# Eight experts' two-layer products on one core: x of four experts in one load, wider transposes, evictions moved to ScalarE

## The chip, the core and the metric

The kernel runs on one core of a Trainium2 chip. A core has TensorE (PE, with a part of its own for loading weights, PEld), VectorE (DVE), ScalarE (ACT), GpSimd (POOL) and SyncE (SP), each with its own instruction queue that is worked off in order, and 16 DMA engines that move data between HBM and the on-chip memory SBUF. Transfers are issued by SP, ACT or POOL. Those from SP and ACT are called hardware_dynamic in the profile (queues q1 and q10), those from POOL software_dynamic (queue q0); in this kernel POOL's transfers of x and of the weights read fp32 and write fp16. Matrix products are summed in PSUM, from where ACT or DVE copies them out.

The metric is the time of one execution in microseconds. A separate profiled execution gives the trace; its span, from the first to the last instruction, is somewhat shorter than the time measured around it.

## What is computed

```python
n_experts, capacity, hidden, expert_hidden = 8, 256, 512, 2048
h = np.matmul(x, w1) + b1[:, np.newaxis, :]
h = np.maximum(h, 0)
return (np.matmul(h, w2) + b2[:, np.newaxis, :]).astype(np.float32)
```

x is 8 x 256 x 512 (4 MB in fp32), w1 is 8 x 512 x 2048 and w2 8 x 2048 x 512 (32 MB each), the output 4 MB. Each weight is used for 256 tokens of one expert only.

## The kernel before

**Tiles.** Everything is multiplied in fp16. POOL's transfers read fp32 weights and write fp16: `load_w1(e)` (line 82) and `load_w2(e)` (line 88) fill [128, 8192] tiles of 2 MB each, from pools of three buffers (lines 48 and 49); the w2 of experts 6 and 7 is loaded in two halves. Weight rows lie on partitions so that each partition reads one contiguous piece of HBM.

**First product.** `first_product(e)` (line 114) makes hT, the hidden layer with hidden units on partitions: for each of 16 groups j, four matmuls of 128x256 into a PSUM tile `ph` (line 121), then one ACT activation with bias and Relu into hT (line 128). It needs x transposed, xT (two buffers), which `transposes(e)` (line 95) makes on DVE in blocks of 32x32, and b1T, the bias b1 transposed by DVE (line 208). The transposes of expert e + 1 are put into the program after the activation j = 8 of expert e (line 135).

**Second product.** `second_product(e)` (line 166) runs three experts later (LAG = 3): for each of two token blocks, a bias matmul with a row of ones (line 171) and 16 matmuls of 128x512 (line 178) into `po0` and `po1`. `store` (line 142) evicts: DVE copies po0 (line 156), ACT copies po1 (line 157). For experts 0 to 3 and 4 to 5 the results are gathered in one tile each, so that a partition holds tokens of one expert that are neighbours in HBM (8 and 4 of them); these two stores are issued by POOL after all weights (`flush`, line 138). Experts 6 and 7 are stored by SP and ACT (line 164). A gathered expert's tokens are evicted in `split` parts of 128/`split` partitions: four of 32 partitions, or two of 64.

**x.** Experts 0 and 1 come by two SP loads of 512 KB in fp32 (line 190), two tokens (4 KB) to a partition, and DVE casts each (line 201). Experts 2 and 3 come by one POOL load, with four tokens to a partition, and experts 4 to 7 by another, with eight (`load_x`, line 72, with `X_LOADS`). The number of tokens on a partition, R, gives the form of the transposes: with R = 2 DVE transposes 32x256 and writes neighbours (line 109); with R = 4 it is 32x256 written at a step of two elements, with R = 8 32x512 at a step of four (line 112). Because the columns of xT then stand in another order than the rows of the output want, the activation at line 128 reads `ph` at a step of `split` and writes hT in runs.

**Order.** PE's matmuls and POOL's transfers keep the order of the program. The main loop (line 227) puts, for step s, the first product of expert s and the second of expert s - 3. The list `ring` (line 215) tells at which step POOL's transfers are put: w1 of expert s and w2 of expert s - 3 at step s - 2, with x loads ahead of w1. POOL's queue is thus: w1 of expert 0, b2, b1, w1 of 1, x of 2 and 3, w1 of 2; then w1 of 3 (which needs the buffer of expert 0, so the end of its first product), w2 of 0, x of 4 to 7; then w1 of 4, w2 of 1, and so on to w2 of 7 and the two flushes. DVE's queue at the start is: the cast and the transposes of expert 0, the cast of expert 1, seven of its transposes, the four transposes of b1T, the rest. ACT's first activation waits for b1T, and its table of functions is loaded after that wait.

Of the kernel before, what the change touches and what calls it, by code (L numbers as in the profile page):

```python
# [10 lines left out]
def kernel(  # L11
# [9 lines left out]
    nc = tc.nc  # L21
    fp32 = mybir.dt.float32
    fp16 = mybir.dt.float16
    E, T, H = x.shape
    M = w1.shape[2]
    P = 128
    nTB = T // P
    nKC = H // P
    nJ = M // P
    B = 32  # L30
    nB = P // B
# [5 lines left out]
    HALVED = (E - 2, E - 1)  # L37


    PARTS = {E - 2: ((0, 25, False), (25, 121, True), (121, 128, False))}  # L40
    nXF32 = 2
    X_LOADS = {2: 2, 4: 4}

    def ordered(ins):
        return tc.keep_in_program_order(ins)
# [3 lines left out]
    w2_pool = ctx.enter_context(tc.tile_pool(name="w2", bufs=3))  # L49
    x_pool = ctx.enter_context(tc.tile_pool(name="xp", bufs=1))  # L50
# [3 lines left out]
    out_pool = ctx.enter_context(tc.tile_pool(name="outp", bufs=2))  # L54
# [3 lines left out]
    ones1 = singles.tile([1, P], fp16)  # L58
# [4 lines left out]
    x16 = [None] * E  # L63
    xT = [None] * E
    w1_sb = [None] * E
    w2_sb = [None] * E
    hT = [None] * E
    pending = {}
    results = {}
    group_of = {first + i: (first, n) for first, n in GROUPS.items() for i in range(n)}  # L70

    def load_x(first, n):

        R = n * T // P
        t = x_pool.tile([P, R, H], fp16, tag=f"x{first}", name=f"x{first}")
        ordered(nc.gpsimd.dma_start(  # L76
            out=t, in_=x[first : first + n].rearrange("e (p r) h -> (e p) r h", r=R)
        ))
        for i in range(n):
            x16[first + i] = (t, i * (P // n), R)  # L80

    def load_w1(e):
        w1_sb[e] = w1_pool.tile([P, nKC, M], fp16, tag="w1", name="w1sb")
        ordered(nc.gpsimd.dma_start(  # L84
            out=w1_sb[e], in_=w1[e].rearrange("(p kc) m -> p kc m", kc=nKC)
        ))

    def load_w2(e):
# [3 lines left out]
        for lo in range(0, nJ, half):  # L92
            ordered(nc.gpsimd.dma_start(out=w2_sb[e][:, lo : lo + half], in_=src[:, lo : lo + half]))  # L93

    def transposes(e):


        t, p0, R = x16[e]
        n = R // nTB
        xT[e] = xT_pool.tile([P, nKC, T], fp16, tag="xT", name="xT")  # L100
        for g in range(T // R // B):
            src = t[p0 + B * g : p0 + B * (g + 1)]
            for b in range(nB):
                block = src[:, :, b * (H // nB) : (b + 1) * (H // nB)].rearrange(
                    "p (n tb) (i kc) -> p tb kc n i", tb=nTB, kc=nKC)
                out = xT[e][b * B : (b + 1) * B].rearrange(
                    "p kc (tb g i n) -> p tb g kc n i", tb=nTB, i=B, n=n)
                if n == 1:
                    nc.vector.transpose(out=out[:, :, g, :, 0, :], in_=block[:, :, :, 0, :])  # L109
                    continue  # L110
                for tb in range(nTB):
                    nc.vector.transpose(out=out[:, tb, g], in_=block[:, tb])  # L112

    def first_product(e):
        hT[e] = hT_pool.tile([P, nJ, T], fp16, tag="hT", name="hT")
        split = group_of[e][1] if e in group_of else 1
        for j in range(nJ):
            bias_at = j * B + e * nB + nB - 1
            ph = psum_h.tile([P, T], fp32, tag="ph", name="ph")
            for kc in range(nKC):  # L120
                ordered(nc.tensor.matmul(  # L121
                    out=ph,
                    lhsT=w1_sb[e][:, kc, :].rearrange("p (q j) -> p q j", j=nJ)[:, :, j],
                    rhs=xT[e][:, kc, :],
                    start=(kc == 0),
                    stop=(kc == nKC - 1),
                ))
            nc.scalar.activation(  # L128
                out=hT[e][:, j, :].rearrange("p (tb k i) -> p tb k i", tb=nTB, k=split),
                in_=ph.rearrange("p (tb i k) -> p tb k i", tb=nTB, k=split),  # L130
                func=mybir.ActivationFunctionType.Relu,
                bias=b1T[:, bias_at : bias_at + 1],
                scale=1.0,
            )
            if j == nJ // 2 and e + 1 < E:
                transposes(e + 1)
# [5 lines left out]
    def store(e, po):  # L142
        if e in group_of:
            first, n = group_of[e]
            split, rows = n, P // n
            if e == first:
                results[e] = group_pool.tile(
                    [P, split * nTB, H], fp32, tag=f"out{e}", name=f"out{e}")
        else:
            first, n, split, rows = e, 1, 1, P  # L150
            results[e] = out_pool.tile([P, nTB, H], fp32, tag="out", name="out")
        out_sb = results[first]
        at = (e - first) * rows
        for k in range(split):
            part = slice(k * rows, (k + 1) * rows)
            nc.vector.tensor_copy(out=out_sb[at : at + rows, k * nTB, :], in_=po[0][part])  # L156
            nc.scalar.copy(out=out_sb[at : at + rows, k * nTB + 1, :], in_=po[1][part])  # L157
        dst = out[first : first + n].rearrange("e (p r) h -> (e p) r h", r=split * nTB)
        if e in group_of:
            if e == first + n - 1:  # L160
                pending[first] = (dst, out_sb)
            return
        for p0, p1, scalar in PARTS.get(e, ((0, P, False),)):
            (nc.scalar if scalar else nc.sync).dma_start(out=dst[p0:p1], in_=out_sb[p0:p1])

    def second_product(e):
        po = []
        for tb in range(nTB):
            t = psum_o.tile([P, H], fp32, tag=f"po{tb}", name=f"po{tb}")
            po.append(t)  # L170
            ordered(nc.tensor.matmul(  # L171
                out=t, lhsT=ones1, rhs=b2_sb[0:1, e * H : (e + 1) * H], start=True, stop=False,
            ))
        half = nJ // 2 if e in HALVED else nJ
        for lo in range(0, nJ, half):
            for tb in range(nTB):
                for j in range(lo, lo + half):
                    ordered(nc.tensor.matmul(  # L178
                        out=po[tb],
                        lhsT=hT[e][:, j, tb * P : (tb + 1) * P],  # L180
                        rhs=w2_sb[e][:, j, :],
                        start=False,
                        stop=(j == nJ - 1),
                    ))
        store(e, po)

    x32 = []
    for e in range(nXF32):
        x32.append(out_pool.tile([P, nTB, H], fp32, tag="out", name="x32"))
        nc.sync.dma_start(out=x32[e], in_=x[e].rearrange("(p tb) h -> p tb h", tb=nTB))  # L190
    load_w1(0)
    ordered(nc.gpsimd.dma_start(  # L192
        out=b2_sb,
        in_=b2.rearrange("e h -> (e h)").rearrange("(o f) -> o f", o=1),
    ))
    ordered(nc.gpsimd.dma_start(out=b1_rows, in_=b1.rearrange("e (b i) -> (e b) i", b=nB)))  # L196
    nc.vector.memset(ones1, 1.0)  # L197

    for e in range(nXF32):
        t = x_pool.tile([P, nTB, H], fp16, tag=f"x{e}", name=f"x{e}")  # L200
        nc.vector.tensor_copy(out=t, in_=x32[e])  # L201
        x16[e] = (t, 0, nTB)
        if e == 0:
            transposes(e)


    for b in range(nB):
        nc.vector.transpose(  # L208
            out=b1T[b * B : (b + 1) * B, nB - 1 - b : nB - 1 - b + nJ * B],
            in_=b1_rows.rearrange("r (i j) -> r j i", j=nJ),  # L210
# [4 lines left out]
    ring = []  # L215
    for s in range(1, E + LAG - 1):
        if s < E:
            if s in X_LOADS:
                ring.append((s - 2, load_x, (s, X_LOADS[s])))
            ring.append((s - 2, load_w1, (s,)))  # L220
        if s >= LAG:
            ring.append((s - 2, load_w2, (s - LAG,)))
# [4 lines left out]
    for s in range(E + LAG):  # L227
        while ring and ring[0][0] <= s:
            _, put, args = ring.pop(0)
            put(*args)  # L230
        if s < E:
            first_product(s)
        if s >= LAG:
            second_product(s - LAG)
# [31 lines left out]
```

## Time and profile before

| | |
|---|---|
| time, median of 3 runs | 181.92 us (181.6 to 182.36) |
| span of the profiled execution | 179.8 us |
| mean granted TensorE clock | 0.932 |
| PE busy / DVE busy / ACT busy / POOL busy | 129.0 / 87.8 / 70.2 / 13.4 us |
| HBM read / written | 71.39 / 4.19 MB |
| moved by the DMA engines (as written) | 40.56 MB |

How to read the lines shown below. The slices are 40 equal parts of the span (or of a window), and each digit is the busy share in tenths, 9 for 90% or more. A line of the timeline gives the start in us, the duration in us, the engine, the line of the code, the operation, output and input with their shapes, how many instructions of one kind stand together, and in brackets how long the engine had been idle and what released it. SPq, POOLq and ACTq are the queues that issue transfers. A line of a group gives the count, the busy time in us and the mean of one in ns, then the idle time before them in us and its releasers. A line of a DMA queue gives the packets, the MB written and the share of the time of 16 engines that these packets took; a packet counts in the window in which it starts, so a short window can show more than 100%.

### The profile page before, as it was taken

How to read it: one execution, taken by the hardware profiler on the slowest of the kernel's cores; microseconds unless marked ns; L12 is line 12 of the kernel's file. 1: busy time of each engine (PE TensorE's matmuls, PEld its weight loads, DVE VectorE, ACT ScalarE, POOL GpSimd, SP SyncE). 2: the span in 40 equal slices, each digit the busy share in tenths (PEclk: the TensorE clock that was granted, in tenths of full speed). 3: DMA queues.
4: the chain of work that ended last, by engine and by line, in shares of the span. 5: the costliest groups of instructions: out<-in, count | busy, mean ns of one | idle time of the engine just before them, and what ended most of it. 6: DMA issues, size and time to landing. Idle time of an engine off the chain costs nothing.

```text
span 179.8 us, 1957 instructions
## 1 busy us (share of the span) xinstructions
PE 129.0 (72%) x784; PEld 86.2 (48%) x784; DVE 87.8 (49%) x125; ACT 70.2 (39%) x151; POOL 13.4 (7%) x28
## 2 busy tenths in 40 slices
PE   0005199959995930999869597969788887999740
PEld 0004089948993410794369244943387433343310
DVE  1999933985000199999999998000600020301010
ACT  0000569947993050482189005940298020111010
POOL 7000003020201010001000001000100020020000
PEclk9999999987999995599999799996999999999995
DMA  5999999999999999999999999999999999999995
GB/s 215 252 230 195 233 208 201 233 228 200 215 231 193 219 230 222 197 226 230 208 204 230 219 200 226 230 211 200 230 219 201 226 211 208 217 211 221 324 456 215
DMA packets 3828, 40.56 MB, mean 226 GB/s; under 512 B 460, under 2 KB 476, under 8 KB 1132
## 3 DMA queue, kind: packets, MB, share of 16 engines
q0 software_dynamic: 3232, 38.35, 96.5%
q1 hardware_dynamic: 476, 1.70, 2.4%
q10 hardware_dynamic: 112, 0.39, 0.5%
q8 instruction: 6, 0.10, 0.2%
q14 instruction: 2, 0.02, 0.0%
HBM read 71.39 MB, written 4.19 MB: 420 GB/s over the span
## 4 chain that ended last, share of the span: by engine, by line
DMA 55%; PE 32%; ACT 3%; another core or an unknown queue 3%; POOL 2%; issue 1%; POOLq 0%; ACTq 0%
DMA w1sb<-in_w_dram 43%; PE po L178 16%; PE ph L121 15%; DMA w2sb<-in_w_dram 12%; ACT out L157 3%; PE po L171 1%; POOL w1sb L84 1%; ACT hT L128 1%; POOL w2sb L93 0%; POOL x L76 0%; POOL b_sb L192 0%; POOL b_rows L196 0%; POOLq L250 0%; ACTq L128 0%
## 5 line engine op out<-in xcount | busy, mean ns | idle before, releaser
L121 PE MATMUL ph<-xT,w1sb 128*128 128x256 f16 x512 | 64.9, 293 | 34.1 <-DMA w1sb<-in_w_dram 21.5
L121 PEld LDWEIGHTS <-w1sb 128*128 128x128 f16 x512 | 59.8, 147 | 40.1 <-DMA w1sb<-in_w_dram 31.8
L178 PE MATMUL po<-w2sb,hT 128*128 128x512 f16 x256 | 60.0, 394 | 9.8 <-DMA w2sb<-in_w_dram 9.8
L112 DVE STREAM_TRANSPOSE xT<-x 32x256 f16<-32x256 f16 (+1 forms) x64 | 53.0, 888 | 26.0 <-DMA x<-in_x_dram 19.2
L128 ACT ACTIVATE hT<-ph,b1T 128x256 f16<-128x256 f32 x128 | 56.2, 474 | 14.4 <-PE ph L121 14.2
L178 PEld LDWEIGHTS <-hT 128*128 128x128 f16 x256 | 25.5, 101 | 44.1 <-issue 17.8
L156 DVE COPY out<-po 32x512 f32<-32x512 f32 (+2 forms) x22 | 15.1, 688 | 53.7 <-PE po L178 53.5
L157 ACT COPY out<-po 32x512 f32<-32x512 f32 (+2 forms) x22 | 12.7, 579 | 68.8 <-PE po L178 68.6
L109 DVE STREAM_TRANSPOSE xT<-x 32x256 f16<-32x256 f16 x32 | 14.0, 436 | 0.5
L93 POOL DMA_DIRECT2D w2sb<-in_w_dram x10 | 5.3, 534 | 71.6 <-PE po L178 71.6
L84 POOL DMA_DIRECT2D w1sb<-in_w_dram x8 | 4.8, 601 | 64.1 <-PE ph L121 63.3
L128 ACT ACT_TABLE_LOAD x1 | 1.3, 1283 | 20.1 <-DVE b1T L208 20.1
L171 PE MATMUL po<-b_sb,ones 1*128 1x512 f16 x16 | 4.8, 379 | 0.0
L208 DVE STREAM_TRANSPOSE b1T<-b_rows 32x512 f32<-32x512 f32 x4 | 4.1, 1031 | 0.1
L201 DVE CAST x<-x 128x1024 f16<-128x1024 f32 x2 | 1.4, 694 | 3.1 <-DMA x<-in_x_dram 3.1
L171 PEld LDWEIGHTS <-ones 1*128 1x128 f16 x16 | 0.9, 92 | 2.1 <-issue 2.1
L140 POOL DMA_DIRECT2D out_dram<-out x2 | 1.1, 538 | 9.8 <-ACT out L157 9.8
L76 POOL DMA_DIRECT2D x<-in_x_dram x2 | 1.1, 552 | 0.0
L197 DVE MEMSET ones<- 1x128 f16 x1 | 0.2, 165 | 0.8 <-PEq L250 0.8
L196 POOL DMA_DIRECT2D b_rows<-in_b_dram x1 | 0.5, 515 | 0.0
L192 POOL DMA_DIRECT2D b_sb<-in_b_dram x1 | 0.5, 513 | 0.0
L250 POOL MEMSET const-float32-0.0<- 128x1 f32 x1 | 0.1, 99 | 0.2 <-issue 0.2
(3 smaller groups left out, 0.3 us busy)
## 6 DMA issues: line engine op xcount, KB each, us to landing
w1sb<-in_w_dram POOLq DMA_DIRECT2D x8, 2048.0 KB, 34.8
w2sb<-in_w_dram POOLq DMA_DIRECT2D x6, 2048.0 KB, 47.2
w2sb<-in_w_dram POOLq DMA_DIRECT2D x4, 1024.0 KB, 23.2
out_dram<-out POOLq DMA_DIRECT2D x1, 2048.0 KB, 19.0
x<-in_x_dram SPq DMA_DIRECT2D x2, 512.0 KB, 3.7
x<-in_x_dram POOLq DMA_DIRECT2D x1, 1024.0 KB, 31.2
out_dram<-out POOLq DMA_DIRECT2D x1, 1024.0 KB, 14.9
x<-in_x_dram POOLq DMA_DIRECT2D x1, 512.0 KB, 24.0
```

What stands on the lines that cost most here:

```text
L84: ordered(nc.gpsimd.dma_start(out=w1_sb[e], in_=w1[e].rearrange("(p kc) m -> p kc m", kc=nKC)))
L93: ordered(nc.gpsimd.dma_start(out=w2_sb[e][:, lo : lo + half], in_=src[:, lo : lo + half]))
L109: nc.vector.transpose(out=out[:, :, g, :, 0, :], in_=block[:, :, :, 0, :])
L112: nc.vector.transpose(out=out[:, tb, g], in_=block[:, tb])
L121: ordered(nc.tensor.matmul(out=ph, lhsT=w1_sb[e][:, kc, :].rearrange("p (q j) -> p q j", j=nJ)[:, :, j], rhs=xT[e][:, kc, :], start=(kc == 0),
L128: nc.scalar.activation(out=hT[e][:, j, :].rearrange("p (tb k i) -> p tb k i", tb=nTB, k=split), in_=ph.rearrange("p (tb i k) -> p tb k i", ...
L156: nc.vector.tensor_copy(out=out_sb[at : at + rows, k * nTB, :], in_=po[0][part])
L157: nc.scalar.copy(out=out_sb[at : at + rows, k * nTB + 1, :], in_=po[1][part])
L171: ordered(nc.tensor.matmul(out=t, lhsT=ones1, rhs=b2_sb[0:1, e * H : (e + 1) * H], start=True, stop=False,))
L178: ordered(nc.tensor.matmul(out=po[tb], lhsT=hT[e][:, j, tb * P : (tb + 1) * P], rhs=w2_sb[e][:, j, :], start=False, stop=(j == nJ - 1),))
L201: nc.vector.tensor_copy(out=t, in_=x32[e])
L208: nc.vector.transpose(out=b1T[b * B : (b + 1) * B, nB - 1 - b : nB - 1 - b + nJ * B], in_=b1_rows.rearrange("r (i j) -> r j i", j=nJ),)
```

## The change

x of experts 0 to 3 is loaded by one SP transfer of 2 MB in fp32: expert e on partitions 32e to 32e + 31, eight tokens to a partition. The target `x32` takes a buffer of the w2 pool and has 16 unused floats after each two tokens, so that the transfer is in rows of 4 KB. One DVE cast makes fp16 of it. POOL's load of experts 2 and 3 is gone; that of 4 to 7 stays. A transpose now takes all eight tokens of a partition: 32x1024, four to an expert, written contiguously; for experts 4 and 5 32x512, eight to an expert, at a step of two. The order of xT's columns changes with it, so the activation reads and writes plainly for experts 0 to 5 and permutes for experts 6 and 7 (reading `ph` at a step of 64). ACT evicts both halves of experts 0 to 5; DVE keeps po0 of experts 6 and 7. In ACT's queue the copies of po0 stand ahead of those of po1. The memset of the row of ones moves from DVE to POOL, behind the load of b1. In DVE's queue the cast and four transposes of expert 0 come first, then the four of b1T, then the other experts'.

```diff
-    nXF32 = 2
-    X_LOADS = {2: 2, 4: 4}
+    XG = P // B
+    GAP = 16
+    R = XG * T // P
+    ON_VECTOR = HALVED
...
+    def rows_of(first):
+        return x[first : first + XG].rearrange("e (p r) h -> (e p) r h", r=R)
+
+    def x_tile(first):
         t = x_pool.tile([P, R, H], fp16, tag=f"x{first}", name=f"x{first}")
-        ordered(nc.gpsimd.dma_start(
-            out=t, in_=x[first : first + n].rearrange("e (p r) h -> (e p) r h", r=R)
-        ))
-        for i in range(n):
-            x16[first + i] = (t, i * (P // n), R)
+        for i in range(XG):
+            x16[first + i] = t[i * B : (i + 1) * B]
+        return t
+
+    def load_x(first):
+        ordered(nc.gpsimd.dma_start(out=x_tile(first), in_=rows_of(first)))
...
+    def split_of(e):
+        return group_of[e][1] if e in group_of else 1
+
     def transposes(e):
-        t, p0, R = x16[e]
-        n = R // nTB
+        s = 2 if split_of(e) == 2 else 1
         xT[e] = xT_pool.tile([P, nKC, T], fp16, tag="xT", name="xT")
...
+        for b in range(nB):
+            src = x16[e][:, :, b * (H // nB) : (b + 1) * (H // nB)].rearrange(
+                "p (s r) (i kc) -> p s kc r i", s=s, kc=nKC)
+            out = xT[e][b * B : (b + 1) * B].rearrange("p kc (r i s) -> p s kc r i", i=B, s=s)
+            for k in range(s):
+                nc.vector.transpose(out=out[:, k], in_=src[:, k])
...
+            columns = ph
+            hidden = hT[e][:, j, :]
+            if split_of(e) == 1:
+                columns = ph.rearrange("p (n tb i) -> p tb i n", tb=nTB, i=B)
+                hidden = hidden.rearrange("p (tb i n) -> p tb i n", tb=nTB, i=B)
             nc.scalar.activation(
-                out=hT[e][:, j, :].rearrange("p (tb k i) -> p tb k i", tb=nTB, k=split),
-                in_=ph.rearrange("p (tb i k) -> p tb k i", tb=nTB, k=split),
+                out=hidden,
+                in_=columns,
...
-            nc.vector.tensor_copy(out=out_sb[at : at + rows, k * nTB, :], in_=po[0][part])
-            nc.scalar.copy(out=out_sb[at : at + rows, k * nTB + 1, :], in_=po[1][part])
+            for tb in range(nTB):
+                to = out_sb[at : at + rows, tb * split + k, :]
+                if tb == 0 and e in ON_VECTOR:
+                    nc.vector.tensor_copy(out=to, in_=po[tb][part])
+                else:
+                    nc.scalar.copy(out=to, in_=po[tb][part])
...
-    x32 = []
-    for e in range(nXF32):
-        x32.append(out_pool.tile([P, nTB, H], fp32, tag="out", name="x32"))
-        nc.sync.dma_start(out=x32[e], in_=x[e].rearrange("(p tb) h -> p tb h", tb=nTB))
+    x32 = w2_pool.tile([P, R // nTB, nTB * H + GAP], fp32, tag="w2", name="x32")[:, :, : nTB * H]
+    nc.sync.dma_start(out=x32, in_=rows_of(0).rearrange("p (n tb) h -> p n (tb h)", tb=nTB))
...
-    nc.vector.memset(ones1, 1.0)
-
-    for e in range(nXF32):
-        t = x_pool.tile([P, nTB, H], fp16, tag=f"x{e}", name=f"x{e}")
-        nc.vector.tensor_copy(out=t, in_=x32[e])
-        x16[e] = (t, 0, nTB)
-        if e == 0:
-            transposes(e)
+    nc.gpsimd.memset(ones1, 1.0)
+
+    nc.vector.tensor_copy(
+        out=x_tile(0).rearrange("p (n tb) h -> p n (tb h)", tb=nTB), in_=x32)
+    transposes(0)
...
-            if s in X_LOADS:
-                ring.append((s - 2, load_x, (s, X_LOADS[s])))
+            if s % XG == 0:
+                ring.append((s - 2, load_x, (s,)))
```

More of the change, by code (lines that the diff above doesn't have):

```diff
@@ L70 @@
     group_of = {first + i: (first, n) for first, n in GROUPS.items() for i in range(n)}
-    def load_x(first, n):
-        R = n * T // P
+    def rows_of(first):
+        return x[first : first + XG].rearrange("e (p r) h -> (e p) r h", r=R)
+    def x_tile(first):
         t = x_pool.tile([P, R, H], fp16, tag=f"x{first}", name=f"x{first}")
-        ordered(nc.gpsimd.dma_start(
-            out=t, in_=x[first : first + n].rearrange("e (p r) h -> (e p) r h", r=R)
-        ))
-        for i in range(n):
-            x16[first + i] = (t, i * (P // n), R)
+        for i in range(XG):
[3 more added lines that the diff above has]
+        ordered(nc.gpsimd.dma_start(out=x_tile(first), in_=rows_of(first)))
     def load_w1(e):
@@ L93, in load_w2 @@
             ordered(nc.gpsimd.dma_start(out=w2_sb[e][:, lo : lo + half], in_=src[:, lo : lo + half]))
+    def split_of(e):
+        return group_of[e][1] if e in group_of else 1
     def transposes(e):
-        t, p0, R = x16[e]
-        n = R // nTB
+        s = 2 if split_of(e) == 2 else 1
         xT[e] = xT_pool.tile([P, nKC, T], fp16, tag="xT", name="xT")
[L101 to L112, printed above, removed]
+        for b in range(nB):
[4 more added lines that the diff above has]
+                nc.vector.transpose(out=out[:, k], in_=src[:, k])
     def first_product(e):
         hT[e] = hT_pool.tile([P, nJ, T], fp16, tag="hT", name="hT")
-        split = group_of[e][1] if e in group_of else 1
         for j in range(nJ):
```

## The prediction

> **What bounds the kernel now.** I read the page first: the busy shares by slice and the chain that ended last.
>
> ```profile
> span 179.8 us, 1957 instructions
> ...
> PE   0005199959995930999869597969788887999740
> ...
> DMA  5999999999999999999999999999999999999995
> ...
> DMA 55%; PE 32%; ACT 3%; another core or an unknown queue 3%; POOL 2%; issue 1%; POOLq 0%; ACTq 0%
> ```
>
> The 16 DMA engines are 90% busy or more in every slice but the first and last; PE has holes everywhere. The end is set by the bytes moved: a microsecond in which the DMA engines have nothing to do is a microsecond on the end, and work on another engine costs nothing unless it delays the issue of a transfer until the queue has run dry. So the question is where the queue has least in reserve. The timeline of the first 48 us:
>
> ```profile
> 0.74 0.87 SPq L190 DMA_DIRECT2D x<-in_x_dram  x2
> ...
> 1.25 0.67 POOL L84 DMA_DIRECT2D w1sb<-in_w_dram  x1 [0.80 <-POOLq L250]
> ...
> 4.09 0.69 DVE L201 CAST x<-x 128x1024 f16<-128x1024 f32 x1 [3.10 <-DMA x<-in_x_dram]
> 4.82 7.18 DVE L109 STREAM_TRANSPOSE xT<-x 32x256 f16<-32x256 f16 x16
> ...
> 15.29 2.78 PE L121 MATMUL ph<-xT,w1sb 128*128 128x256 f16 x12 [15.29 <-DMA w1sb<-in_w_dram]
> 15.90 4.17 DVE L208 STREAM_TRANSPOSE b1T<-b_rows 32x512 f32<-32x512 f32 x4
> ...
> 20.14 1.28 ACT L128 ACT_TABLE_LOAD   x1 [20.14 <-DVE b1T L208]
> ...
> 29.93 0.53 POOL L84 DMA_DIRECT2D w1sb<-in_w_dram  x1 [25.03 <-PE ph L121]
> 30.45 0.54 POOL L93 DMA_DIRECT2D w2sb<-in_w_dram  x1
> 30.98 0.55 POOL L76 DMA_DIRECT2D x<-in_x_dram  x1
> ...
> 47.66 6.98 PEld L121 LDWEIGHTS <-w1sb 128*128 128x128 f16 x64 [0.38 <-DMA w1sb<-in_w_dram]
> ```
>
> The load of w1 of expert 3 needs the buffer of expert 0, so POOL waits 25.03 us for the first product of expert 0, and everything behind it in POOL's queue (w2 of expert 0, x of experts 4 to 7) waits with it. It is issued at 29.93 and lands at 47.66. A load of 2 MB with nothing ahead of it takes about 10.4 us (w1 of expert 0: from the last x packet, about 4.9, to PE's start at 15.29), so its packets begin near 47.66 - 10.4 = 37.3. The reserve is 7.4 us between issue and first packet; this is what a late start of expert 0 eats. The last weights have more (rows further down): w2 of expert 7 is issued at 147.22 and lands at 169.3, 22 us for two halves that take some 10.
>
> **Part 1: x of experts 0 to 3 in one load.** Two SyncE loads of 512 KB become one of 2 MB; POOL's load of experts 2 and 3 (1 MB in fp32) is gone. Bytes from HBM are the same, so DMA work is unchanged to about 0.1 us. What changes is when expert 0 can start: the cast needs all four experts. The queues of the first microseconds, in windows 1 to 3 (40 slices of 0.05), 3 to 4.5, 4.5 to 5 and 5 to 14 us:
>
> ```profile
> GB/s 0 0 0 0 0 0 0 0 0 0 0 0 0 0 0 246 82 0 0 0 0 0 82 328 164 246 573 164 328 655 246 410 655 246 410 573 246 492 573 246
> ```
> ```profile
> DMA packets 168, 0.62 MB, mean 415 GB/s; under 512 B 16, under 2 KB 16, under 8 KB 168
> ...
> q1 hardware_dynamic: 168, 0.62, 102.9%
> ```
> ```profile
> q0 software_dynamic: 16, 0.26, 251.4%
> q1 hardware_dynamic: 35, 0.08, 39.7%
> ```
> ```profile
> q0 software_dynamic: 112, 1.84, 95.8%
> ```
>
> A 4 KB x packet takes 1.5 x 1.029 x 16 / 152 = 0.16 us on its engine (0.62 MB are 152 of them, the rest are semaphores); a w1 packet of 16 KB in fp16 takes 9 x 0.958 x 16 / 112 = 1.23 us. Before, an engine has 16 x packets and 8 of w1; no w1 packet starts until x is through, though w1 was issued at 1.25. After, it has 32 of x. Served alone they end 16 x 0.16 = 2.6 us later, near 7.5; with 0.3 until the semaphore is seen, x lands at 7.8. But w1 becomes ready somewhere ahead of 4.7, and how two queues then share is seen at the other end, where stores of 4 KB packets were issued at 164.81 into a full q0. Windows 164.8 to 168.3 and 169 to 171:
>
> ```profile
> q0 software_dynamic: 106, 0.79, 100.5%
> ...
> out_dram<-out ACTq DMA_DIRECT2D x1, 384.0 KB, 8.1
> ```
> ```profile
> q0 software_dynamic: 68, 0.56, 65.7%
> q10 hardware_dynamic: 62, 0.25, 30.8%
> q1 hardware_dynamic: 18, 0.07, 8.0%
> ```
>
> The newcomer first waits for what the engines already hold (3.5 us, 106 packets or 6.6 an engine; about 1 us of it is the store's own latency, as x's first traffic, at 1.75, came 1 us after 0.74), then the queues take turns: 62 packets of one against 68 of the other, although a packet of q0 is twice as long. ACT's six packets an engine, 1 us of work, landed 8.1 us after issue. By turns, an x packet behind the reserve pays 1.23 us for each w1 packet let in. How many of the 32 are ahead of w1 when it arrives is the unknown. Low end: 16, what the trace shows going first. High end: all 32, no turns. In between there is a plateau: with 8 to 13 packets left, all eight of w1 of expert 0 get in, and the biases' small packets and semaphores behind them cost almost nothing. I take that: x lands at 7.8 + 8 x 1.23 = 17.6.
>
> The Trainium skill (DMA: Bandwidth & Descriptors, Queues, rings and completion order) says that an engine drains a packet of typically 9 to 17 descriptors, at most 64, from one ring before it turns to the next. With turns of that size w1's eight would go in once, at the same 9.8 us; with one of 33 for x there would be none, which is the first rival. The store that needed 8.1 us speaks against such long turns.
>
> **From x to w1 of expert 3.** Durations by form:
>
> ```profile
> L112 DVE STREAM_TRANSPOSE xT<-x 32x512 f16<-32x512 f16 x32 | 40.3, 1331 | 19.8 <-DMA x<-in_x_dram 19.2 <-PE ph L121 0.3
> L109 DVE STREAM_TRANSPOSE xT<-x 32x256 f16<-32x256 f16 x32 | 14.0, 436 | 0.5
> L112 DVE STREAM_TRANSPOSE xT<-x 32x256 f16<-32x256 f16 x32 | 12.7, 444 | 6.2 <-PE ph L121 6.0
> L201 DVE CAST x<-x 128x1024 f16<-128x1024 f32 x2 | 1.4, 694 | 3.1 <-DMA x<-in_x_dram 3.1
> L197 DVE MEMSET ones<- 1x128 f16 x1 | 0.2, 165 | 0.8 <-PEq L250 0.8
> ```
>
> The cast is four times as long: 4 x 0.694 = 2.8 at most, 2.3 if 0.165 of each is a fixed part; I take 2.6. A transpose of 32x1024 isn't in the trace. By the nearest row (436 ns for 256, written contiguously as the new one) it is 1.74, with a fixed part of 0.165 1.25, by the 1331 row (written at a step of four) 2.66. Four of them: 5.0 to 10.6; the contiguous row is nearest: 6.6. Then, in DVE's order, b1T: 4.17. From its end (20.07) to POOL's issue (29.93) 9.86 pass, with ScalarE's table load, the first product and its activations in it. Sum: 17.6 + 2.6 + 6.6 + 4.2 + 9.9 = 40.9 for the issue of w1 of expert 3, 11 us later than before. From issue to first packet lie at least 1.0 (SyncE's load) and at most 3.4 (w1: 1.25 to 4.7); I take 2.0. So packets begin at 42.9 where the engines run dry at 37.3: 5.6 us idle. By the ends of cast, transposes and start-up it is 2.7 to 11. Later loads have reserve to spare, so the gap stays as it is: 179.8 + 5.6 = 185.4 of span. The runs' median lies 2.1 above the span, so 187.5.
>
> **The other edits, each at nothing.** Rows of the stages in the middle:
>
> ```profile
> 62.27 18.84 DVE L112 STREAM_TRANSPOSE xT<-x 32x512 f16<-32x512 f16 x15 [19.18 <-DMA x<-in_x_dram]
> ...
> 72.18 9.26 PEld L121 LDWEIGHTS <-w1sb 128*128 128x128 f16 x64 [8.28 <-DMA w1sb<-in_w_dram]
> ```
> ```profile
> 107.35 2.79 DVE L156 COPY out<-po 32x512 f32<-32x512 f32 x4
> 109.72 0.57 ACT L157 COPY out<-po 32x512 f32<-32x512 f32 x1 [10.61 <-PE po L178]
> ```
> ```profile
> 147.22 1.06 POOL L93 DMA_DIRECT2D w2sb<-in_w_dram  x2 [16.62 <-PE po L178]
> ...
> 149.54 7.07 PE L178 MATMUL po<-w2sb,hT 128*128 128x512 f16 x32 [2.09 <-DMA w2sb<-in_w_dram]
> ...
> 169.36 3.61 PE L178 MATMUL po<-w2sb,hT 128*128 128x512 f16 x16 [1.11 <-DMA w2sb<-in_w_dram]
> ```
> ```profile
> L128 ACT ACTIVATE hT<-ph,b1T 128x256 f16<-128x256 f32 x128 | 56.2, 474 | 14.4 <-PE ph L121 14.2
> ```
>
> The transposes of experts 4 and 5 (eight of 32x512 at a step of two, 0.87 each by the 444 row) and of 6 and 7 become shorter. Expert 4's would end some 3 us earlier than 72.2; there w1 lands at 72.18 anyway, so it gains nothing. Four more copies on ScalarE cost 2.3 us an expert. They need only the first half of the rows (VectorE copies it from 107.35, before the product ends) and stand ahead of the others in ScalarE's order; ScalarE is idle for 10.61 us there, some 4 of it after that half is ready. Without this cover PE would lose 2.3 us at each of four experts and 1.2 at two, against waits for weights of about 2 us a stage (2.09 here) and the reserve of w2 of expert 7: under 1 us would reach the end. The ones on POOL (0.17) stand ahead of a load that has 10 us of queue in front. x in a w2 buffer makes w2 of expert 2, issued at 48.34, wait for a cast that is over by 21.
>
> **The rivals.**
> 1. x goes through whole, as it did before, or w1 comes so late that fewer than four packets are left. Then x lands at 7.8, transposes end at 17.0, b1_rows lands 2.5 later than 15.9, b1T ends at 22.6, and w1 of expert 3 is issued at 32.5. Its packets would be ready at 34.5, 2.8 ahead of the dry point: no idle DMA, 182.0. For it: not one w1 packet came between x's in the window of 3 to 4.5. Against it: the turns at the end. It decides from x landing before about 12.
> 2. Only 16 packets go ahead: after eight turns with w1 of expert 0 and about five with small ones three more fall among w1 of expert 1, and x lands at 21.5: 9.5 idle, 191.4; with no small turns 27.4 and 197. For it: 6.6 packets an engine were all that the stores waited for. Against: those were long packets; in bytes they are as many as 16 to 20 of x.
> 3. The activations of experts 6 and 7 now read PSUM at a step of 64 columns. The trace has steps of 1, 2 and 4, all 0.47. For it: that step is the longest by far. Against: 1, 2 and 4 cost the same. At twice the time, PE loses about 7.6 in each of two first products; some 8 of the 15 are taken up by waits for weights (about 2 a stage), PE ends near 180 instead of 173.0 and the last store after it: 189. It decides from about 0.6 us each.
> 4. Faster: only if SyncE moves x of experts 2 and 3 in 1.6 us instead of 2.6, which no row supports; 181.0.
>
> **How the numbers follow.** Forecast, by turns on the plateau or just below it: 0.45, own range 184 to 191. Rival 1: 0.33. Rival 2: 0.13. Rival 3: 0.03. Rival 4: 0.06. A change of 0.5% (0.9 us) is what can be told from none. Slower is 0.45 + 0.13 + 0.03 = 0.61, same 0.33, faster 0.06. The range reaches down to rival 1 (181.4) and up to the beginning of rival 2 (191.8); outside are most of rival 4 and half of rival 2 and a little of the forecast's tail.
>
> **What would show it.** Right: q0 and q1 packets together between 5 and 15 us, the cast at 13 to 18, b1T ending near 31, POOL's issue of w1 of expert 3 near 41, and a hole of some 5 us in the DMA row near 40 us, with full slices behind it. Wrong: the cast at 8 and no hole. The transposes show as one row of 32x1024 near 1.65 us; b1T after them keeps 1.03. If the hole is there but later than 60 us, it isn't x but PE (rival 3, or the copies).

## The result and the profile after

The kernel after takes 190.2 us (median of 5 runs, 190.01 to 191.11) against 181.92 before: a ratio of 1.047, with a 95% interval of 1.0448 to 1.0493. The span of its profiled execution is 188.6 us against 179.8.

The page of the kernel after, busy tenths in 40 slices of 4.7 us, and its chain that ended last by line:

```profile
span 188.6 us, 1896 instructions
...
PE   0000005599999789089976998595949895999970
...
DMA  5999999806999999999999999999999999999995
...
DMA w1sb<-in_w_dram 23%; DMA w2sb<-in_w_dram 22%; PE po L186 16%; PE ph L120 13%; DMA x<-in_x_dram 11%; DVE xT L112 3%; DVE b1T L211 2%; DVE x L206 1%; PE po L179 1%; ACT L132 1%; ACT out L165 0%; POOL w2sb L97 0%; ACT hT L132 0%; POOL w1sb
```

There is one hole in the DMA row, in the ninth slice, and full slices behind it. The transfer of x, which wasn't on the chain before, now holds 11% of it, and VectorE's three steps behind it 6%. The start in the timeline of the kernel after:

```profile
0.74 0.63 SPq L197 DMA_DIRECT2D x<-in_x_dram  x1
1.26 0.67 POOL L88 DMA_DIRECT2D w1sb<-in_w_dram  x1 [0.81 <-POOLq L253]
...
18.25 0.14 PEld L120 LDWEIGHTS <-w1sb 128*128 128x128 f16 x1 [18.25 <-DMA w1sb<-in_w_dram]
21.64 2.29 DVE L206 CAST x<-x 128x4096 f16<-128x4096 f32 x1 [21.64 <-DMA x<-in_x_dram]
23.96 4.98 DVE L112 STREAM_TRANSPOSE xT<-x 32x1024 f16<-32x1024 f16 x4
28.97 4.21 DVE L211 STREAM_TRANSPOSE b1T<-b_rows 32x512 f32<-32x512 f32 x4
29.00 2.72 PE L120 MATMUL ph<-xT,w1sb 128*128 128x256 f16 x12 [29.00 <-DVE xT L112]
...
33.26 1.28 ACT L132 ACT_TABLE_LOAD   x1 [33.26 <-DVE b1T L211]
...
43.52 0.53 POOL L88 DMA_DIRECT2D w1sb<-in_w_dram  x1 [39.35 <-PE ph L120]
```

x, issued first of all at 0.74, is seen by the cast at 21.64, after w1 of expert 0 (18.25). POOL issues w1 of expert 3 at 43.52 instead of 29.93. How the queues shared the engines shows in the window of 7 to 15 us of the kernel after, by queue (packets, MB, share of 16 engines):

```profile
q0 software_dynamic: 96, 1.57, 92.0%
q1 hardware_dynamic: 95, 0.39, 12.8%
```

96 packets of w1 against 95 of x: one by one, although a packet of w1 holds an engine about seven times as long (92.0% of the time against 12.8%). That the turns are of one packet, and not of several, shows in the DMA row of the window of 5 to 14 us (40 slices of 0.225):

```profile
DMA  9999999304999303999303999603699903699903
```

Its pattern repeats every six slices, 1.35 us; one packet of w1 and one of x take 1.23 + 0.16 = 1.39 us. The size of the hole is read from stretches of the span, where a DMA share of 1.00 is 16 busy engines (the last two columns are DMA share and GB/s). Before:

```profile
0.00:36.00 36.00, 16.82 (x124) 15.28 (x125) 25.86 (x55) 14.21 (x31) 5.45 (x13) 1.00 0.98 221
36.00:48.00 12.00, 9.84 (x73) 8.67 (x72) 6.52 (x17) 8.32 (x19) 1.24 (x3) 0.86 1.02 218
```

After:

```profile
0.00:36.00 36.00, 3.64 (x17) 2.88 (x18) 14.16 (x12) 2.49 (x4) 3.12 (x10) 1.00 0.96 228
36.00:48.00 12.00, 12.00 (x95) 11.16 (x94) 6.88 (x6) 10.17 (x23) 1.59 (x3) 1.00 0.40 74
```

Between 36 and 48 the engines lose (1.02 - 0.40) x 12 = 7.4 us, and in the first 36 us another (0.98 - 0.96) x 36 = 0.7, which two rounded shares give only to some 0.4. Together that is 8.1 of the 8.8 us by which the span grew.

### The profile page after: what moved, and what is told of

It is laid out like the page before. It is cut to its first block, busy times and chain, and to the rows that moved or that the text cites. A ratio compares the mean times of both kernels' runs of the same rounds, so it can differ in the third digit from the quotient of the medians.

```text
span 188.6 us, 1896 instructions
## 1 busy us (share of the span) xinstructions
PE 129.3 (69%) x784; PEld 87.0 (46%) x784; DVE 48.3 (26%) x47; ACT 82.1 (44%) x171; POOL 12.7 (7%) x28
## 4 chain that ended last, share of the span: by engine, by line
DMA 56%; PE 29%; DVE 6%; issue 4%; ACT 1%; POOL 1%; another core or an unknown queue 0%; ACTq 0%; POOLq 0%
DMA w1sb<-in_w_dram 23%; DMA w2sb<-in_w_dram 22%; PE po L186 16%; PE ph L120 13%; DMA x<-in_x_dram 11%; DVE xT L112 3%; DVE b1T L211 2%; DVE x L206 1%; PE po L179 1%; ACT L132 1%; ACT out L165 0%; POOL w2sb L97 0%; ACT hT L132 0%; POOL w1sb L88 0%
## 5 line engine op out<-in xcount | busy, mean ns | idle before, releaser
L112 DVE STREAM_TRANSPOSE xT<-x 32x1024 f16<-32x1024 f16 (+1 forms) x40 | 40.4, 1028 | 45.8 <-PE ph L120 29.1
L165 ACT COPY out<-po 32x512 f32<-32x512 f32 (+2 forms) x42 | 24.3, 578 | 54.5 <-PE po L186 54.2
L163 DVE COPY out<-po 128x512 f32<-128x512 f32 x2 | 1.4, 692 | 65.7 <-PE po L186 65.7
L206 DVE CAST x<-x 128x4096 f16<-128x4096 f32 x1 | 2.3, 2293 | 21.6 <-DMA x<-in_x_dram 21.6
L84 POOL DMA_DIRECT2D x<-in_x_dram x1 | 0.6, 557 | 0.0
```

The lines of the kernel that those rows point to most:

```text
L112: nc.vector.transpose(out=out[:, k], in_=src[:, k])
L163: nc.vector.tensor_copy(out=to, in_=po[tb][part])
L165: nc.scalar.copy(out=to, in_=po[tb][part])
L206: nc.vector.tensor_copy(out=x_tile(0).rearrange("p (n tb) h -> p n (tb h)", tb=nTB), in_=x32)
```

## The experiments

Eight kernels were run. This table puts the numbers of their traces side by side: when the cast of x starts, when POOL issues w1 of expert 3, the span, the median time, and the ratio to the kernel before measured with them (median 181.75 for the four first, 181.6 for the others). All times are in us.

| kernel | cast | issue of w1 of 3 | span | time | ratio, 95% interval |
|---|---|---|---|---|---|
| before | 4.09 (expert 0) | 29.93 | 179.8 | 181.92 | |
| after | 21.64 | 43.52 | 188.6 | 190.2 | 1.047 (1.0448 to 1.0493) |
| rows_16k | 13.51 | 35.73 | 181.1 | 182.81 | 1.0056 (1.0034 to 1.0077) |
| rows_2k | 37.54 | 58.77 | 203.8 | 206.37 | 1.1355 (1.1323 to 1.1386) |
| biases_first | 21.79 | 38.39 | 183.9 | 186.24 | 1.0249 (1.0215 to 1.0284) |
| b1T_first | 21.61 | 43.20 | 188.6 | 190.24 | 1.0451 (1.0409 to 1.0493) |
| w1_held | 19.00 | 40.66 | 185.9 | 187.53 | 1.0324 (1.0302 to 1.0347) |
| rows_16k_biases_first | 13.28 | 30.69 | 180.3 | 182.31 | 1.004 (1.0025 to 1.0055) |
| evict_only | 4.15 (expert 0) | 29.85 | 180.3 | 181.7 | 1.0009 (0.9999 to 1.002) |
| x_by_pool | none | 33.02 | 180.9 | 182.79 | 1.0065 (1.0048 to 1.0082) |

### Fewer and more packets for the same bytes

The first two change only the size of x's rows. `rows_16k`, on the kernel after:

```diff
-    GAP = 16
+    GAP = 0
```

> The kernel after, with the 16 unused floats taken out of x32, so that a partition's eight tokens are one row of 16 KB: 8 packets of x an engine instead of 32, the same bytes. Theory (packets of the two queues take turns one by one, and each x packet that is still queued when w1 of expert 0 arrives costs one w1 packet of 1.2 us): at most two or three of the eight are left then, x lands at 8 to 12 us instead of 21.6, POOL issues w1 of expert 3 before 35, the DMA engines don't run dry, 181.5 to 183 us. Rival (the single load of 2 MB with one cast is late whatever its rows, because two queues share the engines by bytes or because of the cast and transposes): cast still at 18 or later, about 190.

`rows_2k`, on the kernel after:

```diff
-    x32 = w2_pool.tile([P, R // nTB, nTB * H + GAP], fp32, tag="w2", name="x32")[:, :, : nTB * H]
-    nc.sync.dma_start(out=x32, in_=rows_of(0).rearrange("p (n tb) h -> p n (tb h)", tb=nTB))
+    x32 = w2_pool.tile([P, R, H + GAP], fp32, tag="w2", name="x32")[:, :, :H]
+    nc.sync.dma_start(out=x32, in_=rows_of(0))
...
-    nc.vector.tensor_copy(
-        out=x_tile(0).rearrange("p (n tb) h -> p n (tb h)", tb=nTB), in_=x32)
+    nc.vector.tensor_copy(out=x_tile(0), in_=x32)
```

> The kernel after, with 16 unused floats after each token instead of each second, so that x comes in rows of 2 KB: 64 packets an engine, the same bytes. Theory of turns: what goes ahead of w1 is a fixed amount of bytes, so about twice as many packets are left as after (up to 13 there); after w1 of expert 0 and the small loads the rest falls among w1 of expert 1 and perhaps 2, x lands near 31 to 38 us, the hole grows by 10 to 16, 199 to 207 us. Rival (sharing by bytes, or lateness of the load as such): x lands near 21.6 as after, 190.

With 8, 32 and 64 packets an engine for the same 2 MB, the cast starts at 13.5, 21.6 and 37.5, and the times are 182.81, 190.2 and 206.37. Sharing by bytes, or a lateness of the load as such, would have left all three alike. In the window of 7 to 15 us `rows_2k` has as many packets of x as of w1 too:

```profile
q0 software_dynamic: 96, 1.57, 92.0%
q1 hardware_dynamic: 100, 0.20, 7.5%
```

The cast takes 2.3 us in each, so the cast is not it. `rows_16k` stays 0.56% above before: its issue at 35.73 leaves hardly the time of a restart before the engines run dry. That is a part of it: between 36 and 48 us its DMA share is 0.99 against 1.02 before, some 0.4 us of 1.1. What the rest is was not tested. Neither landing was early enough in the expectation: 13.5 where 8 to 12 was expected, and 37.5 at the upper end of 31 to 38.

What goes ahead of w1 is seen in the windows from 0 to the time at which about half of the engines have begun w1. For the kernel after (0 to 6.2), `rows_16k` (0 to 5.95) and `rows_2k` (0 to 6.2), x's queue has:

```profile
q1 hardware_dynamic: 295, 1.21, 61.4%
```
```profile
q1 hardware_dynamic: 82, 1.34, 67.3%
```
```profile
q1 hardware_dynamic: 572, 1.17, 59.0%
```

That is 18.4 packets of 4 KB an engine, 5.1 of 16 KB and 35.8 of 2 KB: very different counts, but 1.2 to 1.3 MB each time, 73 to 84 KB an engine. What goes ahead is not a number of packets. These three can't tell an amount of bytes from a time, as w1 was issued at 1.25 in each; the runs below that issue it later have more bytes ahead (1.54 and 1.74 MB), so it is not a fixed amount of bytes. What is left behind pays by the packet. After, 13.6 of 32 are left; of 64 it is 28.2, so that the rest falls among the eight packets of w1 of expert 1 and then among those of expert 2.

### Order and delay on the other queues

`biases_first`, on the kernel after:

```diff
-    load_w1(0)
     ordered(nc.gpsimd.dma_start(
         out=b2_sb,
...
     nc.gpsimd.memset(ones1, 1.0)
+    load_w1(0)
```

> The kernel after, with POOL's loads of b2 and b1 and its memset put ahead of the load of w1 of expert 0, which is thus issued about 1.2 us later. Theory of turns: 1.2 us are 7 to 8 x packets an engine that go ahead undisturbed; no more than five are left when w1 arrives, x lands at 8 to 14 us, no idle DMA or under 1 us of it, 181.5 to 183.5. Rival (x is late as such): a shift of w1 by 1.2 us makes at most 1.2 us of difference, 189 to 191.5.

x landed no earlier at all: cast at 21.79 instead of 8 to 14. By 7.45, when half of the engines had begun w1, the window from 0 shows:

```profile
q1 hardware_dynamic: 375, 1.54, 63.5%
q0 software_dynamic: 73, 0.22, 12.8%
```

375 packets are 23.4 an engine, 5.0 more than after where 7 to 8 were expected, so 8.6 were left, more than the eight that fit among w1 of expert 0. The small packets of the biases and their semaphores, among which some could pass in the kernel after, had gone by, and so the end of x, its own semaphore with it, fell among w1 of expert 1. Still the time fell by 4.0 us, for a reason that was not the aim: b1_rows landed at 8.02, and VectorE did b1T under the wait for x.

```profile
8.02 4.13 DVE L211 STREAM_TRANSPOSE b1T<-b_rows 32x512 f32<-32x512 f32 x4 [8.02 <-DMA b_rows<-in_b_dram]
12.23 1.28 ACT L132 ACT_TABLE_LOAD   x1 [12.23 <-DVE b1T L211]
21.79 2.29 DVE L206 CAST x<-x 128x4096 f16<-128x4096 f32 x1 [9.64 <-DMA x<-in_x_dram]
24.12 10.00 DVE L112 STREAM_TRANSPOSE xT<-x 32x1024 f16<-32x1024 f16 x8
...
38.39 0.53 POOL L88 DMA_DIRECT2D w1sb<-in_w_dram  x1 [34.23 <-PE ph L120]
```

These rows are the timeline of `biases_first`. With x as late as after, the issue of w1 of expert 3 comes 5.1 us earlier because b1T and the table load left the chain, and the time falls by 4.0. This is the answer that the next run was meant to give.

`b1T_first`, on the kernel after:

```diff
-    nc.vector.tensor_copy(
-        out=x_tile(0).rearrange("p (n tb) h -> p n (tb h)", tb=nTB), in_=x32)
-    transposes(0)
-
     for b in range(nB):
         nc.vector.transpose(
...
         )
+    nc.vector.tensor_copy(
+        out=x_tile(0).rearrange("p (n tb) h -> p n (tb h)", tb=nTB), in_=x32)
+    transposes(0)
```

> The kernel after, with the four transposes of b1T (4.2 us) ahead of the cast in VectorE's order. x lands as late as after (21.6), but b1_rows lands near 19 and its transposes are done by about 23.3, under the wait for x. Theory (the hole is the chain cast, transposes, b1T, table load, first product, issue of w1 of expert 3, minus the time until the queue runs dry): the issue comes 3.4 us earlier than 43.5, near 40, and the hole and the time shrink by as much, 186 to 187.5 us. Rival (the chain behind x isn't what holds the weights back): 190 as after.

Its premise didn't hold, so it is inconclusive as planned: VectorE's order isn't that of the program here, and b1T came to stand behind the cast and two transposes of expert 0, as the timeline shows.

```profile
21.61 2.29 DVE L212 CAST x<-x 128x4096 f16<-128x4096 f32 x1 [21.61 <-DMA x<-in_x_dram]
23.94 2.48 DVE L112 STREAM_TRANSPOSE xT<-x 32x1024 f16<-32x1024 f16 x2
26.43 4.13 DVE L208 STREAM_TRANSPOSE b1T<-b_rows 32x512 f32<-32x512 f32 x4
```

b1T was still on the chain, the issue came at 43.20, and the time was 190.24.

`w1_held`, on the kernel after:

```diff
+    held = singles.tile([P, 3072], fp32)
+    ordered(nc.gpsimd.memset(held, 0.0))
     load_w1(0)
```

> The kernel after, with nothing left out but a memset of a 128x3072 scratch tile put on POOL ahead of the load of w1 of expert 0: work added, to hold that load back by 2 to 4 us. Theory of turns: after, 13.5 of 32 x packets an engine were left when w1's first packet came at 6.2 us; 13.5 x 0.155 = 2.1 us later they are through, so x lands at about 8 us instead of 21.6, with w1 right behind. w1 of expert 3 is issued near 32 to 34 (b1_rows, near 20, then sets the chain), no hole, 181.5 to 184 us, the upper end if the memset is so long that the engines stand still before w1. Rival (x is late as such, or w1's own landing sets the start): later by the 2 to 4 us, 192 to 194.

Work was added and the kernel became faster than after, 187.53 against 190.2. This excludes the rival (192 to 194). But the size was missed: the cast starts at 19.00, not 8. The memset held the issue of w1 back by 2.07 us, to 3.33. In the window from 0 to 7.35, by which 12 packets of w1 have begun, x has:

```profile
q1 hardware_dynamic: 425, 1.74, 66.9%
```

26.6 packets an engine instead of 18.4: the hold bought 8, not 13.5. The rate that the sum took, 0.155 us a packet, was right. In the part of this window that the hold added, 6.2 to 7.35, x has:

```profile
q1 hardware_dynamic: 107, 0.44, 92.5%
```

That is 1.15 x 0.925 x 16 / 107 = 0.16 us a packet. What the sum had wrong is the length of the delay: w1 was issued 2.07 us later, but its packets came only some 1.15 us later (7.35 against 6.2). Why they follow the issue by 4.0 us here and by 4.9 after is not shown.

The 5.4 packets that were left on average took their turns with w1. At 1.39 us a turn that would end near 7.35 + 5.4 x 1.39 = 14.9. x is there only when its last engine is through, and in the window of 16 to 19 us x's queue still has packets:

```profile
q1 hardware_dynamic: 12, 0.02, 1.8%
```

So some engines had far more left than the average. The views don't tell the engines apart, and why they differ stays open.

What the traces also show is a slow beginning of the single load. In the window of 2 to 4 us the kernel before, whose x comes in two loads, and the kernel after have:

```profile
q1 hardware_dynamic: 197, 0.74, 92.1%
```
```profile
q1 hardware_dynamic: 84, 0.34, 84.8%
```

The single load of 2 MB begins at less than half the rate, and a packet of it holds an engine for 2 x 0.848 x 16 / 84 = 0.32 us. `w1_held`, where w1 was not issued until 3.33, moves 0.37 MB in the same window, so the issue of w1 is not the cause; what is was not tested.

`rows_16k_biases_first` joins the edits of those two kernels.

> The kernel after with both edits that were tried singly: rows of 16 KB and the biases' loads ahead of w1. Theory: 5.1 of 8 packets went ahead with 16 KB rows; with w1 1.2 us later 6 to 7 do, x lands at 10 to 12 us, b1T is out of the chain (done by about 13), w1 of expert 3 is issued at 27 to 29, reserve 6 us or more; no hole and no gain below the bytes either: 181.5 to 182.3. If starting earlier were worth something by itself, it would be below 181.

182.31. The window of 0 to 8.27 us, where half of its engines have begun w1, shows that x was through:

```profile
q1 hardware_dynamic: 137, 2.10, 72.0%
```

2.10 MB are all of x. The cast starts at 13.28 only because b1T (9.12 to 13.25) stands ahead of it on VectorE. Issue at 30.69 where 27 to 29 was expected, no hole, and the time is back within 0.4% of the kernel before, at the upper end of what was expected. Against `rows_16k` the issue is 5.0 us earlier and the time only 0.5 us shorter: with hardly any idle DMA to remove, an earlier issue is worth little. The issue is still later than the 29.93 of before, so whether a start earlier than before's would be worth something was not tested.

### The parts that were costed at nothing

`evict_only`, on the kernel before:

```diff
-            nc.vector.tensor_copy(out=out_sb[at : at + rows, k * nTB, :], in_=po[0][part])
+            if e in HALVED:
+                nc.vector.tensor_copy(out=out_sb[at : at + rows, k * nTB, :], in_=po[0][part])
+            else:
+                nc.scalar.copy(out=out_sb[at : at + rows, k * nTB, :], in_=po[0][part])
```

> The kernel before with only the evictions of experts 0 to 5 moved to ScalarE. Theory: the copies of po0 run in ScalarE's idle time during the second half of the second product, and PE's waits for weights take up the rest: same as before within 0.3%, 181.4 to 182.3. Rival (the copies hold up the activations and thus PE): up to 1 us at the end, 182.5 to 183.

181.7, a ratio of 1.0009 (0.9999 to 1.002): no difference that can be told. In its order of ScalarE, as in the kernel after, the copies of po0 run while PE makes po1. The timeline of the kernel after shows it for expert 1:

```profile
90.76 7.07 PE L186 MATMUL po<-w2sb,hT 128*128 128x512 f16 x32 [0.46 <-DMA w2sb<-in_w_dram]
94.41 2.35 ACT L165 COPY out<-po 32x512 f32<-32x512 f32 x4 [4.13 <-PE po L186]
97.86 2.35 ACT L165 COPY out<-po 32x512 f32<-32x512 f32 x4 [1.11 <-PE po L186]
```

The first four copies end at 96.76, the product at 97.83.

`x_by_pool`, on the kernel after:

```diff
-    x32 = w2_pool.tile([P, R // nTB, nTB * H + GAP], fp32, tag="w2", name="x32")[:, :, : nTB * H]
-    nc.sync.dma_start(out=x32, in_=rows_of(0).rearrange("p (n tb) h -> p n (tb h)", tb=nTB))
+    load_x(0)
     load_w1(0)
...
-    nc.vector.tensor_copy(
-        out=x_tile(0).rearrange("p (n tb) h -> p n (tb h)", tb=nTB), in_=x32)
     transposes(0)
```

> The kernel after, with x of experts 0 to 3 loaded by POOL in fp16 ahead of w1 of expert 0, in the same queue: no SyncE load, no cast, no turns. Theory: in one queue x goes first, lands near 8.5 us, transposes end near 14, and no hole comes at 37; but the first packets start about 1 us later than SyncE's (issue to packet 1.8 us against 1.0 to 1.4), and the DMA engines have nothing else in that time: 182 to 183.2. Rival (x of four experts at once is late as such): 186 or more.

182.79. In one queue there are no turns: x of the same four experts is there at 9.24, and all the other edits of the change stay in.

```profile
9.24 9.99 DVE L112 STREAM_TRANSPOSE xT<-x 32x1024 f16<-32x1024 f16 x8 [9.24 <-DMA x<-in_x_dram]
```

So neither the four experts at once, nor the transposes, nor the evictions make the 4.7%. Besides SyncE's load itself, only the cast is missing here, and it takes 2.3 us. It stays 0.65% behind the kernel before, as expected from a start of the transfers that comes later: its first traffic is at 2.6 us, against 1.75 before. From POOL's issue (1.26) that is 1.4 us. The 1.8 us that the expectation took from issue to packet are shown by no run; in the hole of the kernel after it is 1.2.

## Why the prediction was right

It forecast slower, 187.5 us, by a hole of 5.6 us near 40 us in the DMA row, made by turns between x and w1 of expert 0. The place, the sign and the mechanism were right; the hole was larger, because one term of the sum, the landing of x, was sized 4.0 us too early. By its steps:

1. *The bound, and where the reserve is least.* Right. Over the runs with a hole the time follows the issue of w1 of expert 3 nearly one to one: from the kernel after to `rows_2k` the issue moves by 58.77 - 43.52 = 15.3 us and the time by 206.37 - 190.2 = 16.2. Farthest off is `biases_first`, with 5.1 us of issue for 4.0 of time. The kernel with no hole (issue at 30.69) is level with before but for 0.4%.
2. *Turns, one packet each.* Right: 96 against 95, in a pattern of one and one. Rival 1 falls with the cast at 21.64, and the row sizes settle it against sharing by bytes. By turns of 9 to 17 descriptors, as the Trainium skill has them (DMA: Bandwidth & Descriptors, Queues, rings and completion order), the eight packets of x of `rows_16k` would have fitted in one turn, or, once w1 had its turn, all eight of w1 would have gone in, and x could not have been there before 5.9 + 8 x 1.23 = 15.7. The trace does not agree with either: only 5.1 of the eight had gone ahead when w1 came in, and the cast starts at 13.5.
3. *Where x lands.* This is the term that was mis-sized: 17.6 forecast, 21.6 measured, outside the 13 to 18 that was named as a sign of being right. The plateau was too narrow for what it had to hold. 13.6 packets an engine were left on average where the plateau reached to 13, x's own semaphore needs a turn as well, and x isn't there until the last engine's last packet and semaphore are. The window of 18 to 22 us of the kernel after has, by queue:
```profile
q0 software_dynamic: 72, 0.96, 112.2%
q1 hardware_dynamic: 36, 0.08, 7.1%
```

0.08 MB of x, some 20 of its 512 packets, and its semaphores (36 packets in all) go between 0.96 MB of w1 of expert 1. Rival 2 gave 21.5 for such an end, with 16 packets gone ahead where it was 18.4. For this term rival 2 was the better account, and the 190.2 us lie nearer to its 191.4 than to 187.5. The argument that was held against it doesn't come out of the lines: 0.79 MB ahead of the stores are 49 KB an engine, 12 packets of 4 KB as they were written, and not 16 to 20.

4. *Cast and transposes.* 2.3 and 5.0 us where 2.6 and 6.6 were taken: both at the lower bound, the one with a fixed part of 0.165 us an instruction. These 1.9 us hid half of the miss in x, which was luck: nothing ties them to x.
5. *From b1T's end to the issue.* 9.86 taken over from before; after, 43.52 - 33.18 = 10.3. Sum of 3 to 5: 40.9 forecast, 43.5 measured.
6. *Dry point and restart.* The window around the hole in the kernel after (36 to 48 us, 40 slices of 0.3):

```profile
DMA  2955000000000000000000000000099220099009
```

The engines run dry at 37.2 to 38.2, where 37.3 was forecast, and begin again near 44.7, 1.2 us after the issue where 2.0 was taken. The hole is 7.4 us where 5.6 was forecast: 2.6 more from the later issue, 0.8 less from the restart.
7. *The start.* DMA work was costed as unchanged to about 0.1 us. It grew with the slow beginning of the single load. x's queue from 0 to 22 us after, with all of x, and from 0 to 6 us before, with half of it:
```profile
q1 hardware_dynamic: 528, 2.10, 28.0%
```
```profile
q1 hardware_dynamic: 288, 1.05, 45.4%
```

All of x holds the engines for 22 x 0.280 = 6.2 us; twice the half, 2 x 6 x 0.454, would be 5.4. With this 0.7, the hole of 7.4 and the 0.7 of missing share the 8.8 us of the span are accounted for, as far as rounded shares can tell.
8. *The parts at nothing.* Right for the evictions (`evict_only`). The transposes of experts 4 to 7, the memset and the buffer in the w2 pool were not run singly; with all of them in, `rows_16k_biases_first` is within 0.4% of before. Rival 3 fell in the trace: the activations of the kernel after take 474 ns on the mean, as before, and 477 at most, those of experts 6 and 7 with their step of 64 among them.

## What to carry to other kernels

Where the bytes set the end, ask of each edit at the start which transfer it delays, and follow the chain to the issue that refills the queue; what comes later than the dry point costs its full length. When a load in one queue must be early and a queue of large packets follows on another, its rows decide: what is still queued pays one large packet per packet, so few and long rows, or a place ahead in the same queue, keep it early. A load that gates the start is safer small: the two loads of one expert each that the kernel before had were through before the first packet of w1.

## What the runs showed of the hardware that was not expected

- What is served of a queue before a newcomer gets its turn is not a number of packets: 73 to 84 KB an engine until w1 came in, with packets of 2, 4 and 16 KB. Nor is it a fixed amount of bytes: with w1 issued at 2.54 and 3.33 instead of 1.25 it was 96 and 109 KB. Behind a load of x, w1's packets came 4.0 to 4.9 us after the issue; into the empty queue of the hole they came after 1.2 us.
- One load of 2 MB started by SyncE moves 0.34 MB between 2 and 4 us, where two of 512 KB moved 0.74 MB. The cause was not tested.
- A contiguous transpose of 32x1024 takes 1.24 us, where four of 32x256 took 1.74. Written at a step of two, 32x512 takes 0.72; at a step of four it had taken 1.33. The forms of the kernel after, from its groups (the mean in ns behind the busy time):

```profile
L112 DVE STREAM_TRANSPOSE xT<-x 32x1024 f16<-32x1024 f16 x24 | 29.7, 1236 | 29.4 <-PE ph L120 29.1
...
L112 DVE STREAM_TRANSPOSE xT<-x 32x512 f16<-32x512 f16 x16 | 10.8, 716 | 16.4 <-DMA x<-in_x_dram 16.2
```

From 32x256 (436 ns before) to 32x1024, 768 more columns cost 800 ns, 1.04 ns each, and some 0.17 us are fixed if all columns cost the same.
